# A seven-product gate/up stage with its output sums in PSUM and its engine work in the order of product ends

## The chip, the cores and the metric

The kernel runs on one core of one Trainium2 chip. The metric is device time in microseconds (us), the median of the runs shown. The core has five engines with queues of their own: PE (TensorE, matrix products into PSUM; PEld loads its weights), DVE (VectorE), ACT (ScalarE), POOL (GpSimd) and SP (SyncE), which here only issues DMAs. Engines run in parallel and wait for each other through semaphores.

## The reference

One layer of a hybrid decoder trunk, for 512 prompt tokens and 8 x 4 sample tokens (544 columns in all): adaLN modulation, an input projection that feeds a convolution branch and dilated attention, an output projection, a layer norm, and then the part that matters here:

```python
x = layer_norm(DN_ALPHA * x + (1 + g1) * y, ln1_g, ln1_b)
u = x * (1 + sc2) + sh2
h = (jax.nn.silu(u @ w_gate) * (u @ w_up)) @ w_down
x = layer_norm(DN_ALPHA * x + (1 + g2) * h, ln2_g, ln2_b)
```

`u` is 544 x 1024, `w_gate` and `w_up` are 1024 x 2816, all in fp32.

## The kernel before, in words

Activations lie transposed: 128 channels on the partitions, tokens along the free dimension, in two halves h = 0, 1 of 272 columns (`HC`). For precision each matrix is split into a high part (rounded to fp32r) and a low part (the rest), and a product takes three matmuls: high x high, high x low, low x high. The high part of a weight is made by ACT (`act.copy`, L133 and L1100), the low part by DVE (L134, L1083: weight minus high part). In the profile the weights' tiles are `wr` (raw, loaded by SP at L117), `wh` and `wl`; four raw buffers, three of `wh` and `wl`.

The 2816 columns of gate and up are 22 blocks of 128, called f. A block has a gate weight and an up weight of 8 k-blocks each (`gu[2f]`, `gu[2f+1]`). The f's run in three chunks (0 to 7, 8 to 14, 15 to 21). After each chunk its part of `w_down` is applied, in 8 groups m.

The old way (`mm_group`, L193 on; its matmuls are L199, L200 and L202): 48 matmuls for gate, 48 for up, 96 an f. `gu_evict` (L1012 on) makes silu(gate) x up and splits it into the high and low part of H: a sigmoid on ACT (L1016), two multiplications on DVE (L1018, L1020), a cast on ACT (L1022), a subtraction on DVE (L1024).

The seven-product way (`seven`) treats gate and up, and two halves of u2, as a 2 x 2 block product and does it with seven block products instead of eight, 84 matmuls an f (L1111 to L1113). The units are A11, S1, S2, S3, A12, A22 and S4. A's are blocks of the raw weights; S1 to S4 are sums of blocks, made by POOL (`add_up`, L1073) into three slices of the tile `ss`. The right-hand operands are blocks of u2 and sums of them: S1 and S2 (tile `tb`), S3 and A22 (tile `ta`), made once ahead of the stage from the fp32 tile `tf` by DVE and POOL. The products go into four PSUM buffers, X, Zd, Y and Zc of the pool `pmm`, which has four buffers in all and also holds the old way's results. Three of them are used twice, so the fifth to seventh product add onto what the first to fourth left:

```python
tgt = (X, Zd, Y, Zc, X, Zc, Zd)
after = ((), (p1,), (), (p6,), (p7,), (p2,), (p4,))
```

The steps p1 to p7 and e1, e2 (L1131 on DVE, L1134, L1144, L1150, L1155, L1160 on ACT) add the products up into U2, C22, C21 and C12, which lie in SBUF, and form H. Before, each product is followed in program order by one unit's low part, one POOL sum, one unit's high part (five units ahead, `LEAD`), one step left over from the f before (`rest`) and the steps that belong to that product. The order of the instructions of PE, ACT, DVE and POOL is the program's (a manual schedule), so a step that waits holds up everything behind it on its engine.

f 0 and f 1 are done the old way, half h = 0 first, while layer norm 1 of half 1 (`ln1_gen`, interleaved by `tick`) is still at work, and half 1 afterwards from the same weights (`second`, L1234 to L1236). f 2 is done the old way, f 3 to f 20 by seven products, f 21 the old way. The operands of the seven products are prepared around f 2. In the output projection ahead of it POOL adds high and low part of u2[0] up into `tf` (L1003), and in f 3 and f 4 POOL scales z for the second residual (`idle_work`, L1257). Behind f 21 the weights of the last chunk's `w_down` are split into resident tiles (`wd0`, in the place of `ta` and `tb`), which are allowed once the flag `wd0` is set.

Of the kernel before, what the change touches and what calls it, by code (L numbers as in the profile page):

```python
# [54 lines left out]
def hybrid_step_kernel(ctx: ExitStack, tc: tile.TileContext, I, O):  # L55
# [887 lines left out]
    def ln1_gen(h, stats):  # L943
# [24 lines left out]
        if h == 0:  # L968
            for k in range(8):
                if k % 2 == 0:  # L970
                    yield
# [1 line left out]
                act.activation(out=zk, in_=zk, func=AF.Identity, scale=agb[:, 0, k:k + 1], bias=agb[:, 1, k:k + 1])

    wo = []
    for h in range(2):
        stats = Stats(h, dve)
        for m in range(8):
# [21 lines left out]
            if h == 1 and m == 3:  # L1000
                TF.append(big_tile(0, [128, 4, 4, HC], F32, "tf"))
                for i in range(2):
                    pool.tensor_tensor(out=TF[0][:, i], in0=f32(u2[0][:, 0, 4 * i:4 * i + 4]),  # L1003
                                       in1=f32(u2[0][:, 1, 4 * i:4 * i + 4]), op=ALU.add)
# [59 lines left out]
    def add_up(f, n):  # L1064
        g, u = raw_of(f)
        o = sums[f, n] = own["SS"][:, len(sums) % 3]
        x, y, op = {
            "S1": lambda: (u[:, 0:4], u[:, 4:8], ALU.add),
            "S2": lambda: (sums[f, "S1"], g[:, 0:4], ALU.subtract),
            "S3": lambda: (g[:, 0:4], u[:, 0:4], ALU.subtract),  # L1070
            "S4": lambda: (g[:, 4:8], sums[f, "S2"], ALU.subtract),
        }[n]()
        pool.tensor_tensor(out=o, in0=x, in1=y, op=op)  # L1073
# [4 lines left out]

    def unit_low():
        if los:  # L1080
            f, j = los.pop(0)
# [1 line left out]
            dve.tensor_tensor(out=lo, in0=src_of(f, UNITS[j]), in1=f32(hi), op=ALU.subtract)  # L1083
# [8 lines left out]
    def unit_high(f, j):
        if UNITS[j] == "S4":
            at = (own["S4"][:, 0], own["S4"][:, 1])
        else:
            if j // 2 not in ring:
                ring[j // 2] = (whp.tile([128, 8, 128], F32R, tag="wh", name="wh"), wlp.tile([128, 8, 128], F32R, tag="wl", name="wl"))
            at = tuple(t[:, 4 * (j % 2):4 * (j % 2) + 4] for t in ring[j // 2])
        place[f, j] = at
        act.copy(out=at[0], in_=src_of(f, UNITS[j]))  # L1100
        los.append((f, j))

    def unit(f, j):
        unit_high(f, j)
        unit_low()
# [12 lines left out]
    rest = []  # L1118
    idle_work = []

    def flush():
        while rest:
            rest.pop(0)()

    def seven(f, fi, Hs, coming, hooks):
        X, Zd, Y, Zc = [pmm.tile([128, 512], F32, tag="mm", name="mm") for _ in range(4)]
        s1, U2, C22, C21, C12 = small(tmp, "PT"), small(tmp4, "P"), small(tmp4, "P"), small(tmp, "PT"), small(tmp4, "P")
        sg0, sg1 = small(tmp, "w"), small(tmp, "w")
# [4 lines left out]
        def p1():  # L1133
            act.copy(out=s1, in_=X[:, :HC])  # L1134

        def p6():
            tt(U2, s1, Y[:, :HC], ALU.add)

        def p7():
            tt(C22, U2, Zc[:, :HC], ALU.add)  # L1140
            tt(C22, C22, Zd[:, :HC], ALU.add)

        def p2():
            act.activation(out=sg0, in_=X[:, :HC], func=AF.Sigmoid)  # L1144
            tt(sg0, sg0, X[:, :HC], ALU.mult)

        def p4():
            tt(C21, U2, Zc[:, :HC], ALU.add)
            tt(sg0, sg0, C21, ALU.mult)
            act.copy(out=Hs[0][:, 0, fi], in_=sg0)  # L1150

        def p3():
            tt(Hs[0][:, 1, fi], sg0, f32(Hs[0][:, 0, fi]), ALU.subtract)
            tt(C12, U2, Zd[:, :HC], ALU.add)
            act.activation(out=sg1, in_=C12, func=AF.Sigmoid)  # L1155
# [9 lines left out]
        tgt = (X, Zd, Y, Zc, X, Zc, Zd)
        after = ((), (p1,), (), (p6,), (p7,), (p2,), (p4,))
        for j in range(7):
            product(f, j, tgt[j], j < 4)
            unit_low()
            if j == 0:  # L1170
                add_up(f, "S4")
                if f + 1 in coming:
                    add_up(f + 1, "S1")
# [274 lines left out]
```

## Time and profile before

| what | us |
|---|---|
| median of 3 runs | 1056.51 |
| lowest and highest run | 1055.3, 1056.7 |
| the profiled execution | 1055.41 |
| its span, first to last instruction | 1053.5 |
| f 3 to f 7 by seven products | 679.2 to 737.8 |
| f 8 to f 14 | 785.8 to 867.0 |
| f 15 to f 20 | 909.0 to 977.6 |

The mean granted TensorE clock of the profiled execution is 0.984 of full speed.

Rows of the profile are read so. A group gives line, engine, operation, tile written <- tiles read (buffer numbers left out), the sizes as partitions x elements, and how often; in the view of a line or a tile its durations follow in ns as minimum/median/maximum, in a timeline each row has its start and its duration in us. A row of a window gives its length, the busy time (and number of instructions) of PE, PEld, DVE, ACT and POOL, the granted clock (1.00 is full), the share of the DMA engines and GB/s. A bracket names the idle time of the engine just ahead of the row and who ended it. Matmuls are pipelined and their ends are modelled, so a busy PE may be less than fully at work.

### The profile page before, as it was taken

How to read it: one execution, taken by the hardware profiler on the slowest of the kernel's cores; microseconds unless marked ns; L12 is line 12 of the kernel's file. 1: busy time of each engine (PE TensorE's matmuls, PEld its weight loads, DVE VectorE, ACT ScalarE, POOL GpSimd, SP SyncE). 2: the span in 40 equal slices, each digit the busy share in tenths (PEclk: the TensorE clock that was granted, in tenths of full speed). 3: DMA queues.
4: the chain of work that ended last, by engine and by line, in shares of the span. 5: the costliest groups of instructions: out<-in, count | busy, mean ns of one | idle time of the engine just before them, and what ended most of it. 6: DMA issues, size and time to landing. Idle time of an engine off the chain costs nothing.

```text
span 1053.5 us, 21611 instructions
## 1 busy us (share of the span) xinstructions
PE 988.6 (94%) x8952; PEld 943.6 (90%) x8952; DVE 696.1 (66%) x1181; ACT 461.9 (44%) x910; POOL 260.1 (25%) x295
## 2 busy tenths in 40 slices
PE   4999999999999999999999899799999999998895
PEld 3978999999988989999999898699999899998894
DVE  3422688789786463432229788999449984699487
ACT  3312235445458676444524346544225442345323
POOL 0201010010004402011103645572034421343046
PEclk8999999999999999999999999899999999999998
DMA  9998687696774656899735601056756478457402
GB/s 381 362 386 320 224 312 282 239 343 230 268 299 166 235 211 208 303 370 390 292 141 179 206 1 41 30 191 233 292 204 250 160 285 313 160 182 263 162 10 85
DMA packets 44945, 242.64 MB, mean 230 GB/s; under 512 B 7408, under 2 KB 10736, under 8 KB 37680
## 3 DMA queue, kind: packets, MB, share of 16 engines
q1 hardware_dynamic: 34592, 126.83, 33.5%
q10 hardware_dynamic: 7632, 88.43, 22.6%
q0 software_dynamic: 2624, 26.02, 6.1%
q8 instruction: 70, 1.15, 0.4%
q14 instruction: 27, 0.22, 0.1%
HBM read 231.36 MB, written 97.58 MB: 312 GB/s over the span
## 4 chain that ended last, share of the span: by engine, by line
PE 62%; DVE 23%; ACT 7%; issue 3%; DMA 2%; POOL 2%; ACTq 0%; DVEq 0%; SPq 0%; POOLq 0%
PE mm L199 15%; PE mm L200 14%; PE mm L202 14%; DVE wl L1083 5%; DVE wg L1131 5%; PE mm L1111 2%; PE mm L1112 2%; PE mm L1113 2%; PE od L740 2%; PE Sd L705 2%; PE adaps L334 1%; DMA wr<-in_w_in 1%; DVE mrg L829 1%; ACT wh L1100 1%; PE pt L516 1%
## 5 line engine op out<-in xcount | busy, mean ns | idle before, releaser
L199 PE MATMUL mm<-u,wh 128*128 128x272 f32 x984 | 274.7, 296 | 1.1 <-DVE zsa L993 0.7
L200 PE MATMUL mm<-u,wh 128*128 128x272 f32 x984 | 267.3, 289 | 0.0
L202 PE MATMUL mm<-u,wl 128*128 128x272 f32 x984 | 206.4, 290 | 3.0 <-DVE wl L134 3.0
L199 PEld LDWEIGHTS mm<-u,wh 128*128 128x128 f32 x984 | 186.3, 189 | 15.7 <-issue 11.8
L200 PEld LDWEIGHTS mm<-u,wh 128*128 128x128 f32 x984 | 186.6, 190 | 0.2
L134 DVE TENSOR_TENSOR wl<-wr,wh 128x1024 fp32r<-128x1024 f32 (+2 forms) x98 | 114.0, 1164 | 84.7 <-ACT wh L133 78.3
L202 PEld LDWEIGHTS mm<-u,wl 128*128 128x128 f32 x984 | 155.5, 189 | 3.2 <-DVE wl L134 3.2
L133 ACT CAST wh<-wr 128x1024 fp32r<-128x1024 f32 (+2 forms) x98 | 94.9, 970 | 70.3 <-PE mm L200 50.5
L439 DVE SCALAR_TENSOR_TENSOR convy<-glu,vec,convy 128x512 f32<-128x512 f32 x120 | 95.6, 797 | 2.5
L1073 POOL TENSOR_TENSOR ss<-wr 128x512 f32<-128x512 f32 x36 | 53.1, 1476 | 149.8 <-DMA wr<-in_w_gu 82.3
L200 PE MATMUL mm<-h,wh 128*128 128x272 f32 x240 | 64.7, 288 | 0.0
L199 PE MATMUL mm<-h,wh 128*128 128x272 f32 x240 | 64.5, 286 | 0.0
L1029 DVE SCALAR_TENSOR_TENSOR z<-mm,modT,z 128x272 f32<-128x272 f32 (+1 forms) x48 | 21.7, 479 | 54.1 <-PE mm L202 54.1
L1111 PE MATMUL mm<-ta,wh 128*128 128x272 f32 x144 | 42.9, 298 | 12.9 <-DVE wg L1131 12.7
L1083 DVE TENSOR_TENSOR wl<-wr,wh 128x512 fp32r<-128x512 f32 x54 | 49.4, 920 | 4.6 <-ACT wh L1100 4.3
L1131 DVE TENSOR_TENSOR wg<-wg,mm 128x272 f32<-128x272 f32 x108 | 46.4, 429 | 8.0 <-PE mm L1113 5.9
L637 ACT ACTIVATE qk<-mm,vec 128x272 f32<-128x272 f32 (+1 forms) x48 | 25.9, 627 | 56.5 <-PE mm L202 56.5
L202 PE MATMUL mm<-h,wl 128*128 128x272 f32 x240 | 49.6, 288 | 0.0
L1083 DVE TENSOR_TENSOR wl<-ss,wh 128x512 fp32r<-128x512 f32 x54 | 48.8, 910 | 0.0
L654 POOL DMA_DIRECT2D out_kv<-qk x4 | 2.4, 597 | 182.5 <-ACT qk L637 182.5
L1111 PE MATMUL mm<-u,wh 128*128 128x272 f32 x144 | 42.3, 293 | 4.2 <-DVE sgf L1018 4.2
L199 PEld LDWEIGHTS mm<-h,wh 128*128 128x128 f32 x240 | 45.2, 188 | 0.0
(325 smaller groups left out, 2601.3 us busy)
## 6 DMA issues: line engine op xcount, KB each, us to landing
out_s<-in_c ACTq DMA_DIRECT2D x32, 2044.0 KB, 9.4
wr<-in_w_in SPq DMA_DIRECT2D x60, 512.0 KB, 6.3
wr<-in_w_gu SPq DMA_DIRECT2D x44, 512.0 KB, 4.7
KT<-in_kt SPq DMA_DIRECT2D x24, 792.0 KB, 7.1
VV<-in_vv SPq DMA_DIRECT2D x24, 768.0 KB, 7.5
gb<-in_w_ada POOLq DMA_DIRECT2D x8, 2048.0 KB, 16.6
out_s<-in_c ACTq DMA_DIRECT2D x8, 2032.0 KB, 9.3
ga<-in_w_ada SPq DMA_DIRECT2D x8, 1024.0 KB, 17.5
```

Source lines behind the costliest of these rows:

```text
L133: act.copy(out=hv, in_=raw)
L134: dve.tensor_tensor(out=lv, in0=raw, in1=hv.bitcast(F32), op=ALU.subtract)
L199: pe.matmul(ps[h][:, :HC], lhsT=hi[:, k], rhs=A[h][:, 0, k], start=(k == 0), stop=False)
L200: pe.matmul(ps[h][:, :HC], lhsT=hi[:, k], rhs=A[h][:, 1, k], start=False, stop=False)
L202: pe.matmul(ps[h][:, :HC], lhsT=lo[:, k], rhs=A[h][:, 0, k], start=False, stop=(k == nk - 1))
L439: dve.scalar_tensor_tensor(out=o, in0=src, scalar=sc, in1=o, op0=ALU.mult, op1=ALU.add)
L637: act.activation(out=o, in_=src, func=AF.Identity, bias=V("b_in", col))
L1029: dve.scalar_tensor_tensor(out=zz[:, :n1], in0=ps[:, :n1], scalar=modT[:, 5, m, 0:1], in1=zz[:, :n1], op0=ALU.mult, op1=ALU.add)
L1073: pool.tensor_tensor(out=o, in0=x, in1=y, op=op)
L1083: dve.tensor_tensor(out=lo, in0=src_of(f, UNITS[j]), in1=f32(hi), op=ALU.subtract)
L1111: pe.matmul(ps[:, :HC], lhsT=hi[:, k], rhs=B[:, 0, k], start=(first and k == 0), stop=False, skip_group_check=not first)
L1131: dve.tensor_tensor(out=o, in0=a, in1=b, op=op)
```

## The change

It touches the gate/up stage and what is prepared for it.

- One more f in the old way: f 3 goes through `mm_group` and `gu_evict`; the seven products do f 4 to f 20.
- C22, C21 and C12 move from SBUF into PSUM buffers of the pools `ps_s` and `ps_o`.
- The high parts of A11 and S1 are copied a second time, into PSUM (`twice`, one buffer of `ps_t`), and the low part is computed from that copy.
- S2 and S3 lie side by side and are split by one copy and one subtraction of 1024 columns.
- The order inside `seven` is written out: behind each product stand the steps that its end allows, the unit of f + 1 whose buffer it frees among them. The steps left over from an f (`c12`, `lo0`, `m1`, `hi1`, `lo1`, `a22`) are placed by name in the next one.
- `tf`'s part of u2[0] comes from ACT (a second scaling of z in `ln1_gen`) instead of POOL, and there is one more `yield` ahead of it. t3 and t4 are made by DVE instead of POOL. The scaling of z that was POOL's `idle_work` is done by ACT (`keep`) around f 2 and f 3.
- In the last chunk the flag `wd0` is set ahead of f 21, and the left-over steps of f 20 (`flush`) come behind f 21's gate group. The units of the first f of a chunk are spread a little differently over the down groups m = 5 to 7.

The diff, cut to its core:

```diff
         u2[h] = A
         if h == 0:
+            yield
             for k in range(8):
                 if k % 2 == 0:
                     yield
                 zk = stats.zt(k)
+                act.activation(out=TF[0][:, k // 4, k % 4], in_=zk, func=AF.Identity, scale=G9[:, k, 0:1], bias=B9[:, k, 0:1])
                 act.activation(out=zk, in_=zk, func=AF.Identity, scale=agb[:, 0, k:k + 1], bias=agb[:, 1, k:k + 1])
...
                 TF.append(big_tile(0, [128, 4, 4, HC], F32, "tf"))
-                for i in range(2):
-                    pool.tensor_tensor(out=TF[0][:, i], in0=f32(u2[0][:, 0, 4 * i:4 * i + 4]),
-                                       in1=f32(u2[0][:, 1, 4 * i:4 * i + 4]), op=ALU.add)
...
+        act.copy(out=hi, in_=src_of(f, n))
+        if n == "S2":
+            place[f, 2], place[f, 3] = (hi[:, 0:4], lo[:, 0:4]), (hi[:, 4:8], lo[:, 4:8])
+        else:
+            place[f, j] = (hi, lo)
+        seen = f32(hi)
+        if twice:
+            seen = ps_t.tile([128, 4, 128], F32, tag="t", name="hip")
+            act.copy(out=seen, in_=f32(hi))
+
+        def low():
+            dve.tensor_tensor(out=lo, in0=src_of(f, n), in1=seen, op=ALU.subtract)
...
+        product(f, 0, X, True)
+        later("c12")
+        later("lo0")
+        later("m1")
+        lo = unit_high(f, "S4")
+        lo()
+        later("a22")
+        if nxt:
+            add_up(f + 1, "S1")
+        Zd = bank()
+        product(f, 1, Zd, True)
+        s1 = small(tmp, "PT")
+        act.copy(out=s1, in_=X)
+        later("hi1")
+        if nxt:
+            lo = unit_high(f + 1, "A11", True)
+            later("lo1")
+            lo()
+            add_up(f + 1, "S2")
+            add_up(f + 1, "S3")
+        else:
+            later("lo1")
+        Y = bank()
+        product(f, 2, Y, True)
+        U2 = small(tmp4, "P")
+        if nxt:
+            lo = unit_high(f + 1, "S1", True)
+        tt(U2, s1, Y, ALU.add)
+        if nxt:
+            lo()
+            add_up(f + 1, "S4")
...
+        product(f, 3, Zc, True)
+        C22 = ps_s.tile([128, 512], F32, tag="s", name="c22")[:, :HC]
+        U3 = small(tmp4, "P")
+        tt(U3, U2, Zc, ALU.add)
+        tt(C22, U3, Zd, ALU.add)
+        if nxt:
+            unit(f + 1, "S2")
+        product(f, 4, X, False)
+        act.activation(out=sg0, in_=X, func=AF.Sigmoid)
+        tt(sg0, sg0, X, ALU.mult)
+        if nxt:
+            unit(f + 1, "A12")
...
+        product(f, 5, Zc, False)
+        C21 = ps_o.tile([128, 512], F32, tag="o", name="c21")[:, :HC]
+        tt(C21, U2, Zc, ALU.add)
+        tt(C21, sg0, C21, ALU.mult)
+        if nxt:
+            rest["a22"] = unit_high(f + 1, "A22")
+        act.copy(out=Hs[0][:, 0, fi], in_=C21)
+        product(f, 6, Zd, False)
+        C12 = ps_s.tile([128, 512], F32, tag="s", name="c12")[:, :HC]
+        def c12():
+            tt(C12, U2, Zd, ALU.add)
             act.activation(out=sg1, in_=C12, func=AF.Sigmoid)
+        def lo0():
+            tt(Hs[0][:, 1, fi], C21, f32(Hs[0][:, 0, fi]), ALU.subtract)
+        def m1():
             tt(sg1, sg1, C12, ALU.mult)
+            tt(C22, sg1, C22, ALU.mult)
...
-        wg = [f for f in range(k0, k1) if 3 <= f < 21]
+        wg = [f for f in range(k0, k1) if 4 <= f < 21]
...
             pg = mm_group(w_next(2), u2, 8)
+            for i in range(2):
+                gu_evict({1: second[2 * i]}, {1: second[2 * i + 1]}, H, i)
+            dve.tensor_tensor(out=T["S1"][:, 1], in0=tf[:, 0], in1=f32(T["S1"][:, 0]), op=ALU.subtract)
+            prep_to(pos["use"] + 2)
+            pu = mm_group(w_next(2), u2, 8)
+            dve.tensor_tensor(out=T["S2"][:, 1], in0=tf[:, 3], in1=f32(T["S2"][:, 0]), op=ALU.subtract)
             TA = big_tile(0, [128, 2, 2, 4, HC], F32R, "ta")
             T["S3"], T["A22"] = TA[:, 0], TA[:, 1]
             act.copy(out=T["S3"][:, 0], in_=t3)
-            gu_evict({1: second[0]}, {1: second[1]}, H, 0)
+            keep(0)
+            keep(1)
             dve.tensor_tensor(out=T["S3"][:, 1], in0=t3, in1=f32(T["S3"][:, 0]), op=ALU.subtract)
             act.copy(out=T["A22"][:, 0], in_=t4)
+            keep(2)
+            keep(3)
             own["SS"] = one.tile([128, 3, 4, 128], F32, tag="vT", name="ss")
+            gu_evict(pg, pu, H, 2)
+            prep_to(pos["use"] + 2)
...
+            pg = mm_group(w_next(2), u2, 8)
             dve.tensor_tensor(out=T["A22"][:, 1], in0=t4, in1=f32(T["A22"][:, 0]), op=ALU.subtract)
...
+            unit(f, "A11")
+            unit(f, "S1")
+            add_up(f, "S4")
             pu = mm_group(w_next(1), u2, 8)
+            unit(f, "S2")
+            gu_evict(pg, pu, H, 3)
+            unit(f, "A12")
+            rest["a22"] = unit_high(f, "A22")
...
         if j == 2:
+            res["wd0"] = [big_tile(i, [128, 4, 8, 128], F32R, f"wd0{i}") for i in (0, 1)]
+            flags.add("wd0")
+            pg = mm_group(w_next(), u2, 8)
             flush()
-            pg = mm_group(w_next(), u2, 8)
             pu = mm_group(w_next(), u2, 8)
             gu_evict(pg, pu, H, nf - 1)
             copies(0.8)
-            res["wd0"] = [big_tile(i, [128, 4, 8, 128], F32R, f"wd0{i}") for i in (0, 1)]
-            flags.add("wd0")
```

More of the change, by code (lines that the diff above doesn't have):

```diff
@@ L1051, in hybrid_step_kernel @@
     UNITS = ("A11", "S1", "S2", "S3", "A12", "A22", "S4")
-    LEAD = 5
-    rw, place, los, sums, T, own = {}, {}, [], {}, {}, {}
+    rw, place, sums, T, own = {}, {}, set(), {}, {}
     def rhs_of(n):
@@ L1088, in unit_low, with unit @@
                 load_more()
-                assert pos["prep"] == i
+                assert pos["prep"] == i and (f, "S4") in sums
                 pos["prep"] = i + 2
[L1092 to L1105, printed above, removed]
+        return low
+    def unit(f, n):
+        unit_high(f, n)()
     def product(f, j, ps, first):
@@ L1116, in small, with later @@
         return pool_.tile([128, NT if tag == "w" else 512], F32, tag=tag, name="wg")[:, :HC]
-    rest = []
-    idle_work = []
+    rest = {}
+    def later(name):
+        if name in rest:
+            rest.pop(name)()
     def flush():
[L1122 to L1128, printed above, removed]
+        for n in list(rest):
+            later(n)
@@ L1130, in tt, with seven, bank @@
+    def seven(f, fi, Hs, nxt, hooks):
+        def bank():
+            return pmm.tile([128, 512], F32, tag="mm", name="mm")[:, :HC]
         def tt(o, a, b, op):
             dve.tensor_tensor(out=o, in0=a, in1=b, op=op)
[L1133 to L1154, printed above, removed]
+        sg0, sg1 = small(tmp, "w"), small(tmp, "w")
+        X = bank()
+        product(f, 0, X, True)
[3 more added lines that the diff above has]
+        lo = unit_high(f, "S4")
@@ L1165, in seven @@
[L1165 to L1173, printed above, removed]
-            elif j in (1, 3) and f + 1 in coming:
-                add_up(f + 1, ("S2", "S3")[j // 2])
-            n = j + LEAD
-            if n < 7:
-                unit_high(f, n)
-            elif f + 1 in coming:
-                unit_high(f + 1, n - 7)
-            if rest:
-                rest.pop(0)()
-            for g in after[j]:
-                g()
-            if j in hooks:
-                hooks[j]()
-            if idle_work and j > 2:
-                idle_work.pop(0)()
@@ L1189, in seven, with hi1, lo1 @@
-        rest.extend((p3, e1, e2))
+            tt(C22, sg1, C22, ALU.mult)
+        def hi1():
+            act.copy(out=Hs[1][:, 0, fi], in_=C22)
+        def lo1():
+            tt(Hs[1][:, 1, fi], C22, f32(Hs[1][:, 0, fi]), ALU.subtract)
+        rest.update(c12=c12, lo0=lo0, m1=m1, hi1=hi1, lo1=lo1)
         pos["use"] += 2
@@ L1218, in hybrid_step_kernel, with keep @@
             prep_to(pos["use"] + 1)
-            pool.tensor_tensor(out=t3, in0=tf[:, 3], in1=tf[:, 2], op=ALU.subtract)
+            def keep(k):
+                zk = z[:, k, HC:NT]
+                act.activation(out=zk, in_=zk, func=AF.Identity, scale=agb[:, 0, k:k + 1], bias=agb[:, 1, k:k + 1])
             for i in range(2):
```

81 lines of the change are left out of this document (39 added, 42 removed).

## The prediction, made blind

> **What bounds the kernel now.** I read the page first, then the busy times of stretches that I cut at the changed stage, then single lines and tiles in it. The profiled execution spans 1053.5 us and took 1055.41; the median of the three runs is 1056.51, 0.1% more, so I sum on the profile and take the difference from the median. About 0.2% (2.1 us) is what a measurement of this kernel can tell from no change.
>
> ```profile
> span 1053.5 us, 21611 instructions
> PE 988.6 (94%) x8952; PEld 943.6 (90%) x8952; DVE 696.1 (66%) x1181; ACT 461.9 (44%) x910; POOL 260.1 (25%) x295
> ```
>
> ```profile
> core 0: us, PE busy (x) PEld busy (x) DVE busy (x) ACT busy (x) POOL busy (x), PEclk, DMA share, GB/s
> 679.20:737.80 58.60, 55.28 (x420) 54.62 (x421) 53.38 (x88) 28.30 (x58) 28.53 (x24) 0.97 0.55 197
> 785.80:867.00 81.20, 75.67 (x591) 74.38 (x590) 74.82 (x123) 38.63 (x80) 30.95 (x22) 1.00 0.61 218
> 909.00:977.60 68.60, 64.54 (x506) 63.66 (x505) 62.84 (x105) 33.23 (x68) 24.60 (x18) 1.00 0.60 206
> 977.60:989.70 12.10, 12.10 (x98) 12.04 (x97) 2.91 (x7) 1.66 (x5) 0.00 (x0) 1.00 0.35 127
> 989.70:1005.00 15.30, 12.64 (x87) 12.27 (x86) 9.62 (x14) 6.96 (x9) 0.00 (x0) 0.89 0.46 150
> ...
> ```
>
> ```profile
> 844.10:856.40 12.30, 10.87 (x86) 10.65 (x85) 11.84 (x19) 5.57 (x12) 5.77 (x4) 1.00 0.70 251
> ```
>
> The first three windows are the seven-product f's of the three chunks (5, 7, 6 of them). The fourth is f 21 in the old way: 96 matmuls in 12.1 us, 0.1254 each, nothing else late. Seven products are 84 matmuls, so 10.5 us if PE never waits; the windows give 11.7, 11.6 and 11.4 an f. The single f from 844.1 takes 12.3, PE loses 1.4 there and DVE is busy 11.84. So in this stage DVE is the bound, against a page in which PE leads.
>
> ```profile
> L1131 DVE TENSOR_TENSOR wg<-wg,mm x108: 422/426/441, 685.5 to 978.1; 128x272 f32<-128x272 f32 x108
> L1131 DVE TENSOR_TENSOR wg<-wg x54: 426/442/1537, 690.8 to 979.6; 128x272 f32<-128x272 f32 x54
> L1083 DVE TENSOR_TENSOR wl<-wr,wh x54: 676/688/1777, 674.2 to 968.8; 128x512 fp32r<-128x512 f32 x54
> L1073 POOL TENSOR_TENSOR ss<-wr x36: 1279/1430/2322, 670.3 to 960.6; 128x512 f32<-128x512 f32 x36
> ```
>
> ```profile
> 846.29 2.98 DVE L1131 TENSOR_TENSOR wg<-wg 128x272 f32<-128x272 f32 x2
> ```
>
> ```profile
> 845.84 1.69 POOL L1073 TENSOR_TENSOR ss<-wr 128x512 f32<-128x512 f32 x1 [3.81 <-DMA wr<-in_w_gu]
> 847.61 1.37 POOL L1073 TENSOR_TENSOR ss<-ss,wr 128x512 f32<-128x512 f32 x1
> ```
>
> Durations are min/median/max in ns. A DVE op with one input in PSUM (wg<-wg,mm) never leaves 0.42 to 0.44 in 108 cases; with both inputs in SBUF it reaches 1.54, and a weight's low half 1.78. The two timelines show why: two such multiplications take 2.98 us because each ends where a POOL addition does (847.5, 849.0). Twelve of the 18 DVE ops of an f have both inputs in SBUF, and POOL adds four times an f.
>
> **The change part by part.** *Steady f's.* After the change 4 of 17 DVE ops (the low halves of S4, A22, A12 and of S2 with S3, one op of 1024) read SBUF twice. C22, C21, C12 and second copies of A11's and S1's high halves lie in PSUM.
>
> ```profile
> L1100 ACT CAST wh<-wr x54: 609/620/631, 671.4 to 968.2; 128x512 fp32r<-128x512 f32 x54
> L519 ACT COPY PT<-pt x24: 572/587/682, 178.5 to 410.1; 128x512 f32<-128x512 f32 x24
> L1155 ACT ACTIVATE wg<-wg x18: 431/432/433, 694.3 to 978.6; 128x272 f32<-128x272 f32 x18
> L133 ACT CAST wo<-wr x8: 1036/1045/1054, 565.0 to 590.6; 128x1024 fp32r<-128x1024 f32 x8
> L134 DVE TENSOR_TENSOR h<-wr,h x2: 1212/1218/1225, 636.7 to 653.4; 128x1024 fp32r<-128x1024 f32 x2
> ```
>
> DVE undisturbed: 11 ops of 0.43, 5 of 0.68, one of 1.22, together 9.35: under 10.5. ACT gets two copies more (2 x 0.62); its sum is 4 halves of 0.62, two copies, one of 1.05, six ops of 0.4: 7.2, beside PE. The copy into PSUM is in no row. Nearest are SBUF to SBUF 0.62 and PSUM to SBUF 0.59; I take 0.62; up to 1.2 it stays off the path, because S1's low half has over 1 us before it is missed. ps_t has one buffer, so S1's second copy waits on ACT for A11's low half; behind it stands the copy of S2 and S3, which waits for POOL anyway.
>
> What is late next is a ring through POOL. The S1 addition of f+1 overwrites the slice from which S4 of f is read, so it waits for S4's low half. From that end on: A22's low half 0.60 (POOL waits, since both read SBUF; next ops on one engine start 0.08 before the last ends), three additions at 1.31 and 0.2 of handoffs 4.13, the copy of S2 and S3 1.05 + 0.06, their low half 1.22 + 0.06, sg0 times X 0.35, A12's low half 0.60, C21 0.35 and 0.49, C12 0.35, sigmoid 0.49, two multiplications 0.98, S4's low half 0.60. Sum 11.3 an f. The addition's 1.31 is chosen: 1.28 is its undisturbed minimum, 1.43 its median with two weight inputs; with 1.31 the same laying end to end of before's queues gives 10.5, 11.4, then 12.2, and 10.5 for the last f of a chunk: 81.2 and 69.0 for the windows of 81.2 and 68.6. A chunk enters with its units ready, which puts the ring over a microsecond ahead, and it loses 0.8 an f: two f's of 10.5, a third of 10.9; the last, with no next f, 10.8. Seven f's: 10.5 + 10.5 + 10.9 + 3 x 11.3 + 10.8 = 76.6 against 81.2, so -4.6. Six: 65.3 against 68.6, so -3.3. Bounds: 10.6 if the slack of POOL is better than I think, 12.2 if the S4 addition always gets in ahead of S2's low half. The S4 addition and A22's copy of a chunk's first f move into the down groups m = 6 and 7: nothing, beside 5 to 6 us of PE each.
>
> [...]
>
> *First chunk: one more f in the old way.* It adds 12 matmuls (1.5 us), but what counts is when f 4 starts its products.
>
> ```profile
> 662.30:674.80 12.50, 9.03 (x50) 8.63 (x48) 10.93 (x11) 5.77 (x10) 6.51 (x4) 0.73 0.12 43
> 674.80:679.20 4.40, 0.20 (x2) 0.00 (x0) 4.40 (x6) 1.20 (x3) 3.03 (x3) 1.00 0.00 0
> 679.20:682.60 3.40, 3.39 (x15) 3.39 (x16) 3.26 (x7) 2.59 (x6) 2.02 (x2) 0.50 0.00 0
> ```
>
> ```profile
> 660.71 1.29 DVE L1227 TENSOR_TENSOR tb<-tf,tb 128x1088 fp32r<-128x1088 f32 x1
> 661.97 3.54 DVE L1228 TENSOR_TENSOR tb<-tf,tb 128x1088 fp32r<-128x1088 f32 x1
> 665.43 1.21 DVE L134 TENSOR_TENSOR wl<-wr,wh 128x1024 fp32r<-128x1024 f32 x1
> ```
>
> ```profile
> 691.38 0.29 PE L1111 MATMUL mm<-u,wh 128*128 128x272 f32 x1
> ```
>
> ```profile
> L973 ACT ACTIVATE z<-z,agb x8: 601/602/609, 623.0 to 634.1; 128x272 f32<-128x272 f32 x8
> ```
>
> Before, PE loses 3.5 us to a low half queued behind L1228, which POOL's t4 held for 2.3, waits 4.4 more for the units, and runs at half clock after each idle stretch (0.50 in the third window). f 4 begins at 691.38. After: t3 and t4 are DVE ops of 1.29 and POOL blocks nothing. From 657.2 (L1227's 660.71 less two ops, less 0.8 that t3 on POOL cost) run three of 1.29 at 1.25, the S2 copy 1.1, gu5's copy 1.05 and low half 1.21: it ends at 664.3, not 666.6, and f 2's up group, 45 matmuls on, at 669.9. But f 3's gate group needs the PSUM buffers of f 2's gate group (pmm has four, all held), so it waits for f 2's first two multiplications (L1018), and these for a sigmoid that stands on ACT behind what the change puts there. DVE: two evictions of h = 1 (six ops, two casts and handoffs) 3.6, S1 low, gu6 low, S2 low 3.6, to 671.5. ACT then: S3 copy 1.1 (it overwrites tf, so after S2 low), two keeps of z 1.1, A22 copy 1.1, two keeps 1.1, sigmoid 0.4, to 676.1. The multiplication ends at 676.6. PE idles 6.7, then 96 matmuls 12.0, then half clock on about 26 of them, 2.6. f 4 begins at 691.3: nothing won, nothing lost. Bounds: 688 (no half clock, keeps overlap) to 694.5. Its four f's take 10.6 + 11.0 + 11.3 + 10.8 = 43.7, to 735.1 against 737.8: -2.7.
>
> [...]
>
> *The sums of u2 off POOL.* Two POOL additions go, eight ACT ops of 0.6 come, and one extra yield puts them later.
>
> ```profile
> L1003 POOL TENSOR_TENSOR tf<-u x2: 2525/2528/2531, 616.1 to 623.6; 128x1088 f32<-128x1088 f32 x2
> ```
>
> ```profile
> 616.48 2.44 DVE L950 TENSOR_TENSOR u<-u2a,u 128x272 fp32r<-128x272 f32 x1 [0.53 <-ACT u L960]
> ```
>
> ```profile
> 635.34 0.43 ACT L873 ACTIVATE lnsq<-z 128x272 f32<-128x272 f32 x1 [0.61 <-DVE z L995]
> ```
>
> DVE loses 2.0 to each addition (0.44 alone, 2.44 here), so 4 come back there. On ACT, eight ops at 0.51 start to start, 4.1, now stand ahead of the last square, 635.34. The two cancel: 0, from -1 to +4 if only the ACT side shows.
>
> *The end of the gate/up stage.* The weights of the first down groups are split during f 21 instead of behind it.
>
> ```profile
> 991.01 0.85 ACT wd L133
> ...
> 991.89 1.10 DVE wd L134
> ...
> 993.03 0.48 PE mm L202
> ```
>
> The window from 989.7 holds 84 matmuls of down, 10.5 us, and 2 others, and takes 15.3. Split early, these rows leave the path; H of f 21 is needed only 18 matmuls in, 2.25 us, and its casts end at 991.01, 1.3 after f 21's last matmul. So -4.7, half clock included. Cover: f 21's 12 us.
>
> One call of copies falls away; the last piece moves from f 20 to f 21, off the path.
>
> Sum: -4.6 - 3.3 - 2.7 + 0 - 4.7 = -15.3. Profile 1040.1, median 1041.2.
>
> **The rivals.** *PE becomes the bound* (10.6 an f): the chunks win another 1.3, 2.6 and 1.9: 1035.4. For: POOL's undisturbed 1.28 and DVE's 9.35. Against: the ring's sum.
>
> *Another wait takes the place of the old*, 12.2 an f: the S4 addition ahead of S2's low half, or the weights. Row:
>
> ```profile
> wr<-in_w_gu SPq DMA_DIRECT2D x44, 512.0 KB, 4.7
> ```
>
> The POOL row at 845.84 above waited 3.81 for such a load, so a landing can be far slower than this median; a shorter period leaves it less time. Then the two later chunks lose 0.3 and 0.7, f 4 to 7 (45.2) win 1.2, the end 4.7: 1051.3.
>
> *Slower: POOL stops every DVE op, PSUM or not.* DVE's 9.35 less 17 overlaps of 0.08, 8.0, and four additions, 5.2, then follow one another: 13.2 an f. With 10.7 for a first and 10.8 for a last f, seven take 87.5 (+6.3), six 74.3 (+5.7), four 47.9 (+1.4); with the end's -4.7 that is 1065.2. It turns slower from 12.6 an f on (11 such f's). Against it stand 108 cases of wg<-wg,mm within 20 ns.
>
> *The change does not do what it says* (A11's and S1's low halves still stop, up to 1.31 each, with 1 us of slack): 12 an f, within the second rival.
>
> **How the numbers follow.** Forecast 0.52, own range 1036 to 1046; PE bound 0.20; another wait 0.17; slower 0.05; the rest 0.06 is the ACT side of u2's sums with half clock twice on top of the second rival, 1055 to 1059. The range 1032 to 1052 holds the second rival and the bounds above and leaves out about 0.17: the slower case, the last 0.06 and the far ends. Faster by over 0.2%: 0.52 + 0.20 + 0.17 + 0.01 = 0.90; the same 0.04; slower 0.06.
>
> **What would show it.** Right: PE's idle time ahead of L1111 that DVE wg ends, in all,
>
> ```profile
>   DVE wg L1131: 28.2, 22
> ```
>
> (both PE rows, us and times) falls to a few us; low halves of A11 and S1 stay at 0.68; the S1 addition starts right behind the low halves of S4 and A22; f's of 11.3 in mid chunk; PE idle 6 to 7 us ahead of f 3's gate group, released by sgf; no gap at the first down group. Wrong: f's of 12 with POOL waiting for DMA, or PSUM readers beyond 0.5 us; lnps later than before.

## The result and the profile after

The changed kernel takes 1040.48 us, the median of four runs from 1038.72 to 1041.41; the kernel before ran at 1056.61 beside it. The ratio is 0.984, with a 95% interval from 0.982 to 0.987. The profiled execution took 1039.63 us and spans 1037.9, which is 15.6 less than the 1053.5 of before.

The page of the changed kernel, first lines; the columns are as before:

```profile
span 1037.9 us, 21539 instructions
...
PE 989.9 (95%) x8964; PEld 946.5 (91%) x8964; DVE 647.1 (62%) x1156; ACT 480.8 (46%) x931; POOL 233.5 (23%) x279
```

DVE lost 49 us of busy time with 25 operations fewer, which would be 2 us for each, and the longest DVE operation of this stage takes 1.29 in the changed kernel: the operations that stayed became shorter. ACT gained 19 us.

The busy times by stretch, cut at the same events as before (f 3's gate group, the seven-product f's of the three chunks, f 21, the first down groups of the last chunk):

```profile
core 0: us, PE busy (x) PEld busy (x) DVE busy (x) ACT busy (x) POOL busy (x), PEclk, DMA share, GB/s
...
672.00:678.80 6.80, 0.45 (x5) 0.23 (x3) 3.56 (x5) 4.69 (x8) 2.37 (x2) 0.89 0.22 77
678.80:693.30 14.50, 14.50 (x96) 14.50 (x97) 7.56 (x12) 6.41 (x12) 2.70 (x3) 0.81 0.12 37
693.30:736.80 43.50, 43.17 (x339) 42.53 (x338) 33.91 (x65) 24.85 (x48) 16.39 (x12) 1.00 0.54 192
784.80:860.30 75.50, 75.09 (x591) 74.29 (x590) 59.70 (x117) 44.17 (x85) 32.86 (x24) 1.00 0.65 235
902.30:966.70 64.40, 64.20 (x506) 63.64 (x505) 50.93 (x99) 37.73 (x72) 27.36 (x20) 1.00 0.61 226
966.70:978.80 12.10, 12.10 (x99) 12.10 (x98) 5.50 (x11) 3.54 (x7) 0.00 (x0) 1.00 0.61 205
978.80:989.40 10.60, 10.60 (x86) 10.60 (x86) 7.52 (x12) 5.08 (x7) 0.00 (x0) 1.00 0.47 165
```

Read down the first number behind each stretch. Seven f's take 75.5 us instead of 81.2, six take 64.4 instead of 68.6, the first down groups 10.6 instead of 15.3: 5.7, 4.2 and 4.7 us. The first chunk's four seven-product f's end at 736.8 instead of 737.8, 1.0 earlier, although f 4 starts later, at 693.3 instead of 691.4. These four are the whole 15.6. PE is now busy in 99.5% of the second chunk's stage, where it was at 93%; DVE went from 92% to 79%.

Single lines of the changed kernel (min/median/max in ns), L1136 being the element operations, L1098 the low halves, L1071 POOL's additions:

```profile
L1136 DVE TENSOR_TENSOR c<-wg,c x34: 445/445/447, 705.0 to 971.5; 128x272 f32<-128x272 f32 x34
L1136 DVE TENSOR_TENSOR wg<-wg,c x17: 436/439/440, 706.5 to 971.1; 128x272 f32<-128x272 f32 x17
```

```profile
L1098 DVE TENSOR_TENSOR wl<-wr,hip x14: 686/688/690, 697.7 to 949.8; 128x512 fp32r<-128x512 f32 x14
L1098 DVE TENSOR_TENSOR wl<-ss,hip x14: 686/687/691, 700.1 to 951.9; 128x512 fp32r<-128x512 f32 x14
```

```profile
  DVE wg L1136: 3.6, 13
```

No element operation reaches 0.45 us any more, where the slowest took 1.54, and the low halves that read a high half in PSUM stay within 5 ns of each other. The last fence is the idle time of PE ahead of a product that a DVE operation ended: 3.6 us in 13 places, where it was 28.2 in 22.

### The profile page after: what moved, and what is told of

Its sections match the earlier page's. It is cut to its first block, busy times and chain, and to the rows that moved or that the text cites. A ratio compares the mean times of both kernels' runs of the same rounds, so it can differ in the third digit from the quotient of the medians.

```text
span 1037.9 us, 21539 instructions
## 1 busy us (share of the span) xinstructions
PE 989.9 (95%) x8964; PEld 946.5 (91%) x8964; DVE 647.1 (62%) x1156; ACT 480.8 (46%) x931; POOL 233.5 (23%) x279
## 4 chain that ended last, share of the span: by engine, by line
PE 65%; DVE 11%; issue 8%; ACT 7%; POOL 5%; DMA 4%; ACTq 0%; DVEq 0%; POOLq 0%
PE mm L199 16%; PE mm L200 15%; PE mm L202 15%; POOL ss L1071 3%; DMA wr<-in_w_gu 2%; PE mm L1114 2%; PE mm L1115 2%; PE mm L1116 2%; PE od L740 2%; PE Sd L705 2%; PE adaps L334 1%; PE pt L516 1%; DVE mrg L829 1%; DMA wr<-in_w_in 1%; DVE wl L134 1%
## 5 line engine op out<-in xcount | busy, mean ns | idle before, releaser
L199 PE MATMUL mm<-u,wh 128*128 128x272 f32 x1016 | 285.0, 298 | 6.4 <-DVE sgf L1017 6.4
L200 PE MATMUL mm<-u,wh 128*128 128x272 f32 x1016 | 277.0, 290 | 0.0
L202 PE MATMUL mm<-u,wl 128*128 128x272 f32 x1016 | 213.7, 290 | 0.5 <-DVE wl L134 0.5
L199 PEld LDWEIGHTS mm<-u,wh 128*128 128x128 f32 x1016 | 193.7, 191 | 20.9 <-issue 11.0
L200 PEld LDWEIGHTS mm<-u,wh 128*128 128x128 f32 x1016 | 193.9, 191 | 0.4
L202 PEld LDWEIGHTS mm<-u,wl 128*128 128x128 f32 x1016 | 161.3, 190 | 0.7 <-DVE wl L134 0.7
L133 ACT CAST wh<-wr 128x1024 fp32r<-128x1024 f32 (+2 forms) x100 | 97.0, 972 | 66.5 <-PE mm L200 50.5
L1071 POOL TENSOR_TENSOR ss<-wr 128x512 f32<-128x512 f32 x34 | 50.2, 1476 | 189.0 <-DVE s L1098 90.2
L1087 ACT CAST wh<-ss 128x512 fp32r<-128x512 f32 (+1 forms) x34 | 28.4, 835 | 43.6 <-POOL ss L1071 30.6
L199 PEld LDWEIGHTS mm<-h,wh 128*128 128x128 f32 x240 | 45.2, 188 | 0.0
L200 PEld LDWEIGHTS mm<-h,wh 128*128 128x128 f32 x240 | 45.1, 188 | 0.0
L509 ACT ACTIVATE P<-P,st 128x256 f32<-128x256 f32 x64 | 31.2, 489 | 28.3 <-DVE st L503 25.8
L1114 PE MATMUL mm<-ta,wh 128*128 128x272 f32 x136 | 40.4, 297 | 0.9 <-DVE wg L1136 0.8
L200 PE MATMUL mm<-mrg,wo 128*128 128x272 f32 x128 | 37.9, 296 | 1.8 <-DVE mrg L829 1.7
```

What stands on the lines that cost most here:

```text
L133: act.copy(out=hv, in_=raw)
L199: pe.matmul(ps[h][:, :HC], lhsT=hi[:, k], rhs=A[h][:, 0, k], start=(k == 0), stop=False)
L200: pe.matmul(ps[h][:, :HC], lhsT=hi[:, k], rhs=A[h][:, 1, k], start=False, stop=False)
L202: pe.matmul(ps[h][:, :HC], lhsT=lo[:, k], rhs=A[h][:, 0, k], start=False, stop=(k == nk - 1))
L509: act.activation(out=p[:, a:b], in_=p[:, a:b], func=AF.Exp, bias=st[:, kd, s, hh, 0:1], accum_out=st[:, kd, s, hh, 1:2])
L1087: act.copy(out=hi, in_=src_of(f, n))
```

## Experiments

Each kernel is the changed kernel with one edit (the last two with several), timed against the kernel before on the same chip. Ratios are to the kernel before; the changed kernel's own is 0.984 (0.982 to 0.987), and differences of medians are against its 1040.5. The kernel before took 1057.6 to 1058.2 beside the experiments and 1056.6 beside the changed kernel, so a difference of medians can be off by over a microsecond: by the ratios the gains come out up to 1 us larger and the losses up to 1.3 smaller.

**Is it the place of the operands? All in SBUF.** C22, C21 and C12 go back to SBUF, and the second copies of A11's and S1's high halves go, so seven more operations of an f have both inputs in SBUF; the order of the work stays.

```diff
-        C22 = ps_s.tile([128, 512], F32, tag="s", name="c22")[:, :HC]
+        C22 = small(tmp4, "P")
-        C21 = ps_o.tile([128, 512], F32, tag="o", name="c21")[:, :HC]
+        C21 = small(tmp, "PT")
-        C12 = ps_s.tile([128, 512], F32, tag="s", name="c12")[:, :HC]
+        C12 = small(tmp4, "P")
-            lo = unit_high(f + 1, "A11", True)
+            lo = unit_high(f + 1, "A11")
-            lo = unit_high(f + 1, "S1", True)
+            lo = unit_high(f + 1, "S1")
```

> Changed kernel with its order of work, but C22, C21, C12 in SBUF and no second copies of the high halves of A11 and S1 (four operations of an f read PSUM less; two ACT copies go). Theory: DVE operations with two SBUF inputs stop beside POOL's additions again: f's of about 12.2 us in mid chunk, 1050 to 1053 us, and low halves of A11 and S1 that reach over 1 us. Rival: the order of the work and the merged operation of S2 and S3 made the gain: f's of 10.8 to 11.3, 1039 to 1043 us.

It took 1059.3 us, ratio 1.001 (1.000 to 1.003): 18.9 more than the changed kernel, more than the theory gave, and the whole gain gone with wins elsewhere (the first down groups) still in it. Three f's in the middle of the second chunk, first in the changed kernel, then in this one:

```profile
816.80:849.70 32.90, 32.49 (x254) 31.85 (x254) 26.02 (x52) 19.96 (x39) 16.42 (x12) 1.00 0.61 217
```

```profile
827.80:864.50 36.70, 32.51 (x255) 31.85 (x254) 35.70 (x52) 16.97 (x33) 18.06 (x12) 1.00 0.57 197
```

The same 52 DVE operations are busy 35.7 us instead of 26.0. An f takes 12.2, as expected; what the theory missed is the second f of a chunk, which takes 14.8, 14.2 and 12.7. With these operands in SBUF the new order gains nothing. The converse, the old order with the operands in PSUM, was not run: the place is shown to be needed, not to be enough.

**Which of them: the low halves or the sums?** Two halves of that edit, apart.

> Changed kernel without the second copies of the high halves of A11 and S1: their two low halves read SBUF twice, C22, C21 and C12 stay in PSUM, and two ACT copies (0.59 each, one of them on the ring) go. Theory: what counts is which operations lie beside POOL's additions, and these two do (A11's beside the S1 addition, S1's beside that of S3): each stops for up to 1.3 us, f's of 11.8 to 12.5, 1050 to 1057 us. Rival: the number of operations with two SBUF inputs counts, and these are two of seven that all-SBUF adds: 1040 to 1045 us; below 1040 if the copy on ACT was the dearer way.

> Changed kernel with C22, C21 and C12 in SBUF and the second copies of the high halves kept in PSUM: five more operations of an f read SBUF twice. Theory (place decides): most of them lie between the last product and the low half of S4, when POOL waits for that low half; only the low half of the second H (842.86 us, beside the S1 addition) stops, at most 0.9 an f: 1042 to 1048 us. Rival (number decides): five of the seven operations of all-SBUF's 19 us come back: 1051 to 1056 us.

Without the second copies: 1047.8 us, ratio 0.990 (0.989 to 0.992), 7.3 more. With the three C's in SBUF: 1041.1, ratio 0.985 (0.983 to 0.986), no difference. So place decides and not number, but the sizes were missed: for the low halves the theory's was too high and the rival's too low, and the C's came out 0.9 under their theory's range. The f's of the kernel without copies take 11.6 to 11.8. Its low halves, DVE first, then POOL's additions in the same f:

```profile
812.78 1.43 DVE L1098 TENSOR_TENSOR wl<-wr,wh 128x512 fp32r<-128x512 f32 x1
814.48 1.42 DVE L1098 TENSOR_TENSOR wl<-ss,wh 128x512 fp32r<-128x512 f32 x1
```

```profile
811.99 1.67 POOL L1071 TENSOR_TENSOR ss<-wr 128x512 f32<-128x512 f32 x1 [5.50 <-DVE s L1098]
813.73 1.62 POOL L1071 TENSOR_TENSOR ss<-ss,wr 128x512 f32<-128x512 f32 x1
815.31 1.73 POOL L1071 TENSOR_TENSOR ss<-wr 128x512 f32<-128x512 f32 x1
```

Both engines pay: the low halves take 1.43 instead of 0.69, and POOL's additions 1.6 to 1.7 instead of 1.3. Of the five operations on the C's four lie where POOL waits some 5.5 us for S4's low half, and nothing meets them. The fifth, the low half of the second H, lies beside the S1 addition; with the C's in SBUF it takes 1.52 to 1.54 instead of 0.44 in 11 of the 17 f's:

```profile
842.98 1.53 DVE L1136 TENSOR_TENSOR h<-wg,h 128x272 fp32r<-128x272 f32 x1
```

That costs 0.1 us an f, because DVE was idle for 1.10 a little later, ahead of S1's low half, and that idle time takes most of it up. The two halves cost 7.3 and 0.6 apart and 18.9 together. In the kernel with all in SBUF the same 11 operations stop, but there is no idle time behind them: A11's low half then takes 1.78 instead of 1.43, and the low half of S2 and S3 comes to lie beside the S4 addition and takes 1.78 instead of 1.23.

```profile
845.18 1.78 DVE L1098 TENSOR_TENSOR wl<-wr,wh 128x512 fp32r<-128x512 f32 x1
...
849.38 1.78 DVE L1098 TENSOR_TENSOR wl<-ss,wh 128x1024 fp32r<-128x1024 f32 x1
```

In these rows a low half of 128x512 with both inputs in SBUF takes 1.42 to 1.78 us where it starts while an addition runs, and A22's, which starts ahead of one, 0.68 (at 811.83 in the kernel without copies). With one input in PSUM, the 28 of the changed kernel take 0.686 to 0.691.

**What is the ring of 11 us?** The next f's S1 low half goes behind U2 + Zc.

```diff
         tt(U2, s1, Y, ALU.add)
-        if nxt:
-            lo()
-            add_up(f + 1, "S4")
...
         tt(U3, U2, Zc, ALU.add)
+        if nxt:
+            lo()
+            add_up(f + 1, "S4")
         tt(C22, U3, Zd, ALU.add)
```

> Changed kernel with one move on DVE and POOL: the low half of the next f's S1 (and the S4 addition behind it) comes behind U2 + Zc instead of ahead of it. Theory: the ring that sets 10.8 to 11.05 us in mid chunk runs S4 low, S1 addition 1.29 to 1.68, two copies on ACT 1.25, S1 low 0.69, U2 + Zc 0.43, sixth product; with the last but one off it the f's take 10.55 and the three chunks win 1.1, 1.5 and 1.1: about 1037 us. Rival: the ring of the prediction (three additions in a row, then the copy and low half of S2 and S3) stands right behind it and keeps 10.8 to 11: 1040 to 1041 us.

It took 1036.7 us, ratio 0.981 (0.978 to 0.984), 3.8 less by the medians, though the two intervals overlap. The f's take 10.59 (84 matmuls at 0.1254 are 10.53) until the fifth of a chunk; the last two of the second chunk take 11.06 and 11.03, the last of the third 11.03. So the theory has the place where PE waits, but not what sets 11 us. S4's low half in three f's of this kernel:

```profile
796.17 0.69 DVE L1098 TENSOR_TENSOR s<-ss,s 128x512 fp32r<-128x512 f32 x1
807.22 0.69 DVE L1098 TENSOR_TENSOR s<-ss,s 128x512 fp32r<-128x512 f32 x1
818.27 0.69 DVE L1098 TENSOR_TENSOR s<-ss,s 128x512 fp32r<-128x512 f32 x1
```

They lie 11.05 apart, while PE starts the same f's at 793.30, 803.89 and 814.48, 10.59 apart. A loop that takes 11.05 while PE runs at 10.59 doesn't go through PE: it is the rival's ring, the one of the prediction. From the second f of a chunk on it is 10.8 to 11.1 long in both kernels, and the move leaves it as it is. What the move changes is how far PE gets ahead before it meets the ring: in the f's in which PE waits, S4's low half ends 5.2 us into the f here and 3.7 in the changed kernel. In the last f's a low half of the down weights stands ahead of U2 + Zc as well. The stages won 0.9, 0.5 and 0.3 us, 1.7 of the expected 3.7; f 4 starts 1.2 earlier in this profile for nothing that the edit does, and the rest is within the scatter of the runs.

**The stall ahead of f 3's gate group.** f 2's sigmoids and first multiplications, taken out of `gu_evict` as `gate`, go right behind the evictions of the second halves.

```diff
-            dve.tensor_tensor(out=T["S1"][:, 1], ...
+            sg = gate(pg)
             prep_to(pos["use"] + 2)
             pu = mm_group(w_next(2), u2, 8)
+            dve.tensor_tensor(out=T["S1"][:, 1], ...
+            gu_evict(pg, pu, H, 2, sg)
             dve.tensor_tensor(out=T["S2"][:, 1], ...
...
-            gu_evict(pg, pu, H, 2)
```

> Changed kernel (1040.5 us), with f 2's sigmoid and first multiplication put right behind the evictions of the second halves, ahead of the low halves and of the copies of S3 and A22. Theory: the 6.64 us that PE waits ahead of f 3's gate group is queue order alone; the stall goes to under 1 us, with it the half clock behind it (22 matmuls at 0.23 instead of 0.125, 2.3 us), f 4 starts at 684.5 to 687 instead of 693.3: 1031.5 to 1034 us. Rival: the units of f 4 (low halves of S3 and A22, the sums on POOL) come no earlier, so the wait moves to f 4's first products; f 4's third product starts no earlier than 693: 1037 us or more.

1038.0 us, ratio 0.981 (0.979 to 0.984): 2.5 less, with intervals that overlap, where the theory had 6.5 to 9. The stall is gone from where it was, but PE now waits at f 3's up group, and neither the theory nor the rival had named that:

```profile
682.14 0.39 PE L199 MATMUL mm<-u,wh 128*128 128x272 f32 x1 [3.33 <-ACT wh L133]
```

```profile
679.05 1.08 ACT L1286 CAST ta<-t 128x1088 fp32r<-128x1088 f32 x1
680.04 1.12 ACT L1253 ACTIVATE z<-z,agb 128x272 f32<-128x272 f32 x2
681.06 1.03 ACT L133 CAST wh<-wr 128x1024 fp32r<-128x1024 f32 x1
```

The second fence is ACT's queue: the up weights' high half (L133) stands behind the same copies and scalings that had held the sigmoid. PE then waited once more, ahead of the matmul that needs its low half; by the matmul starts the two waits are 3.6 and 1.9. f 4 starts at 691.5 instead of 693.3.

**The sums of u2, later on ACT.** The eight ACT operations go behind the second half's square root, the scaling of z's first half into the first chunk's down groups.

> Changed kernel with the eight ACT operations that make the sums of u2 moved from ahead of the last square to behind the square root of the second half, and the scaling of z's first half moved into the first chunk's down groups. Theory: the last matmul of the statistics (638.86 us in the changed kernel, PE idle 5.6 ahead of it) waits for the last square behind these operations; it comes at about 634.4, the half clock behind it goes too, and all later work moves up by 4 to 5.5 us: 1035 to 1036.5 us. Rival: the queue of ACT ahead of f 3's gate group takes the gain back, since the same operations then stand before u2's second half: 1039.5 to 1041 us.

1034.1 us, ratio 0.978 (0.975 to 0.980): 6.4 less and 0.9 under the theory's range, the largest gain of these single edits. The last statistics matmul, in the changed kernel and here:

```profile
638.86 0.82 PE L923 MATMUL lnps<-lnq,ones 128*128 128x272 f32 x1 [5.25 <-POOL lnq L882]
```

```profile
635.69 0.50 PE L923 MATMUL lnps<-lnq,ones 128*128 128x272 f32 x1 [0.22 <-POOL lnq L882]
```

PE's idle of 5.25 is 0.22, and f 4 starts at 689.6 instead of 693.3, although the output projection began 1.5 later in this profile (571.5 against 570.0). The wait ahead of f 3's gate group stays at 6.35 us, so the rival is out.

**The sums of u2, back on POOL.**

> Changed kernel with the sums of u2 made on POOL again by two additions, from the high and low halves, and without the eight ACT operations. The prediction's term for this part of the change was 0, from -1 to +4. Theory: of the two sides only ACT's counts, as the last statistics matmul came at 638.86 against 636.91 before: putting it back wins 1.5 to 2.5 us, 1038 to 1039 us. Rival: DVE loses its 4 us beside POOL's additions again and is then late by as much: 1040 to 1043 us.

1037.9 us, ratio 0.982 (0.980 to 0.983), 2.6 less by the medians; the intervals of the two ratios overlap, so this leans to the theory and no more. In its profile the output projection began 1.5 later, as above, and the last statistics matmul comes at 639.4; from one to the other it is 67.9 us, against 68.9 in the changed kernel and 67.1 before, so 1.0 of the 1.8 that the change had added there is gone again. From 608 to 650 us PE lost, in matmul starts later than 0.125 behind the one before, 4.8 us before the change, 8.6 in the changed kernel, 6.4 here, and 2.9 with the later place.

**The tail undone.** The weights of the first down groups are split behind f 21 again.

> Changed kernel with the weights of the first down groups split behind f 21 again. Theory: the prediction's term, 4.7 us (idle 2.3 and 0.9 ahead of the first down group's first and third matmul, half clock on the rest): 1044.5 to 1046 us. Rival: f 21's eviction now comes otherwise, and part of the split hides beside it: 1041 to 1043 us.

1045.2 us, ratio 0.988 (0.986 to 0.989), 4.8 more by the medians, near the term of 4.7. In its profile the stretch from f 21's last matmul to the 82nd of the down groups takes 16.4 us, against 15.0 before and 10.3 in the changed kernel, as 24 matmuls run at half clock there and 16 did before: the matmul between the two waits takes 0.43 (at 981.35), where it took 0.28 before (at 992.14). The waits are back where they were:

```profile
980.95 0.59 PE L199 MATMUL mm<-h,wd 128*128 128x272 f32 x1 [2.46 <-ACT wd L133]
...
982.08 0.59 PE L202 MATMUL mm<-h,wd 128*128 128x272 f32 x1 [0.31 <-DVE wd L134]
```

**f 3 in seven products again.**

```diff
-        wg = [f for f in range(k0, k1) if 4 <= f < 21]
+        wg = [f for f in range(k0, k1) if 3 <= f < 21]
```

(and without f 3's two groups and its eviction)

> Changed kernel with f 3 in the seven-product way again, all else as it is. The prediction held that one more f in the old way wins and loses nothing as far as f 4's start goes. Theory: f 3's first product then waits for the sums on POOL and for ACT's copies and scalings until about 682 to 683, runs its first products at half clock, and f 4 starts at 694 to 696 instead of 693.3: 1041 to 1043.5 us. Rival: PE has 12 matmuls less (1.5 us) and f 3's units are as early as f 3's up group was: f 4 at 691 to 692, 1038 to 1039.5 us.

1040.3 us, ratio 0.983 (0.982 to 0.985): no difference. f 3 starts at 681.6 behind 9.3 us of idle PE, and f 4 at 694.0 against 693.3. So the theory had f 4's start right; the time is 0.7 below its range. One more f in the old way is worth nothing here.

**The gains together.** The three moves, f 3's up weights split right behind f 2's eviction, A11's low half behind U2, and all scalings of z in the down groups.

> Changed kernel with the three moves together: f 2's gate multiplication early (and, as that run left PE waiting 3.6 and 1.9 us for f 3's up weights behind ACT's queue, these weights split right behind f 2's eviction), the sums of u2 behind the second half's square root, U2 and U2 + Zc ahead of the low halves of A11 and S1; all sixteen scalings of z go into the first chunk's down groups. Theory: the gains add: 6.4 (sums of u2), 3.8 to 4.5 (U2 + Zc), 8.7 (stall of 6.6 and half clock 2.3): 1020 to 1023 us. Rival: f 4's sums and low halves then come last and keep f 4's third product waiting: 1025 to 1031 us.

1029.9 us, ratio 0.973 (0.972 to 0.975). The gains didn't add: the time is in the rival's range, but the wait is not the rival's; it is at f 4's first product:

```profile
684.88 0.59 PE L1114 MATMUL mm<-u,wh 128*128 128x272 f32 x1 [4.80 <-DVE sgf L1012]
```

It is the pattern of f 2 once more: a PSUM buffer that f 3's first multiplication holds, and this stands on DVE behind the low half of S2 and S3, which waits for POOL. POOL's sums there, and the first of them in the next kernel:

```profile
676.52 2.27 POOL L1071 TENSOR_TENSOR ss<-wr 128x512 f32<-128x512 f32 x1 [28.50 <-DVE ta L1277]
678.87 1.60 POOL L1071 TENSOR_TENSOR ss<-ss,wr 128x512 f32<-128x512 f32 x1
680.43 1.71 POOL L1071 TENSOR_TENSOR ss<-wr 128x512 f32<-128x512 f32 x1
```

```profile
676.17 1.29 POOL L1071 TENSOR_TENSOR ss<-wr 128x512 f32<-128x512 f32 x1 [28.50 <-DVE ta L1277]
```

The next kernel's edit against this one, cut to its core:

```diff
...
             pg = mm_group(w_next(2), u2, 8)
-            dve.tensor_tensor(out=T["A22"][:, 1], ...
...
-            unit(f, "A11")
-            unit(f, "S1")
-            add_up(f, "S4")
+            lo = unit_high(f, "A11", True)
+            sg = gate(pg)
+            lo()
             pu = mm_group(w_next(1), u2, 8)
+            unit_high(f, "S1", True)()
+            add_up(f, "S4")
+            gu_evict(pg, pu, H, 3, sg)
             unit(f, "S2")
-            gu_evict(pg, pu, H, 3)
+            dve.tensor_tensor(out=T["A22"][:, 1], ...
...
```

> The combined kernel of before (1029.9 us) with f 3's eviction and f 4's first units in another order: in the combined kernel f 4's first product waits 5.1 us for a PSUM buffer that f 3's first multiplication holds behind the low half of S2 and S3, and the next product waits 1.4 more. Here f 3's sigmoids and first multiplications come ahead of f 4's units, A11's and S1's first low halves read a copy in PSUM, the low half of A22's sum moves behind S2 and S3, and in every f C22 is made ahead of S1's low half. Theory (queue order again): f 4 starts at 679.8 to 681 instead of 684.9, its first f takes 10.6 to 11 instead of 12.0: 1023 to 1025.5 us. Rival: POOL's three sums in a row (2.3, 1.6 and 1.7 us there) are the bound and the wait moves to f 4's third product: 1026 to 1029 us.

1026.4 us, ratio 0.971 (0.969 to 0.972): 3% below the kernel before and 1.4% below the changed one. f 4 starts at 679.6, 13.8 us earlier than in the changed kernel, with no idle ahead of it: the theory's place. The time is 0.9 above the theory's range and at the low end of the rival's. POOL's sums are at 1.3 again, and one matmul of the third product starts 0.8 behind the one before, so the rival's wait isn't there. The theory's first f of 10.6 to 11 isn't there either: f 4 to f 7 take 11.6, 11.4, 10.9 and 10.8. They start with their units just made and have no lead to use up; that reason is argued, not tried. PE is busy in 96% of the span.

## Why the prediction held, step by step

It said 1041.2 and it was 1040.5; profile against profile, 1040.1 forecast and 1039.6 measured. The reason was right. That the total comes within 0.7 us is partly luck, because two errors in its terms cancel.

- **DVE operations with two SBUF inputs stop beside POOL's additions, those with one in PSUM don't.** Shown for the operations of this stage: all-SBUF costs 18.9 us with the order kept, and its low halves reach 1.78 us and its element operations 1.53. The rival in which POOL stops every DVE operation is out, since the 28 low halves that read PSUM keep 0.686 to 0.691 us while additions run beside them.
- **Steady f's: the right ring, sized too long.** Forecast 76.6 and 65.3 for the windows, measured 75.5 and 64.4. The pattern is the forecast one: in the second chunk two f's at PE's pace (10.60 and 10.59), one of 10.78 in which the lead runs out, then 11.06, 10.83 and 11.05 where 11.3 stood, and 10.6 for the last where 10.8 stood. The term that was mis-sized is "A22's low half 0.60 (POOL waits, since both read SBUF", with the three additions behind it. One f of the changed kernel, on DVE, POOL, ACT and PE:

```profile
841.66 0.68 DVE L1098 TENSOR_TENSOR s<-ss,s 128x512 fp32r<-128x512 f32 x1
...
845.48 0.69 DVE L1098 TENSOR_TENSOR wl<-ss,hip 128x512 fp32r<-128x512 f32 x1 [1.10 <-POOL ss L1071]
846.09 0.43 DVE L1136 TENSOR_TENSOR wg<-wg,mm 128x272 f32<-128x272 f32 x1
...
847.84 1.23 DVE L1098 TENSOR_TENSOR wl<-ss,wh 128x1024 fp32r<-128x1024 f32 x1 [0.84 <-ACT wh L1087]
...
852.71 0.68 DVE L1098 TENSOR_TENSOR s<-ss,s 128x512 fp32r<-128x512 f32 x1
```

```profile
842.42 1.68 POOL L1071 TENSOR_TENSOR ss<-wr 128x512 f32<-128x512 f32 x1 [5.50 <-DVE s L1098]
844.18 1.30 POOL L1071 TENSOR_TENSOR ss<-ss,wr 128x512 f32<-128x512 f32 x1
845.43 1.28 POOL L1071 TENSOR_TENSOR ss<-wr 128x512 f32<-128x512 f32 x1
```

```profile
846.75 1.05 ACT L1087 CAST wh<-ss 128x1024 fp32r<-128x1024 f32 x1 [1.37 <-POOL ss L1071]
```

```profile
846.57 0.39 PE L1114 MATMUL mm<-ta,wh 128*128 128x272 f32 x1 [0.20 <-DVE wg L1136]
```

S4's low half ends at 842.34, and each step of the ring starts where the one before ends. By the profile the S1 addition doesn't wait for A22's low half to end, as the prediction had it. It starts right behind S4's, takes 1.68 beside A22's, and the third addition ends at 846.71, 4.37 behind S4's low half where 0.60 and 4.13 stood. The copy and the low half of S2 and S3 then take 2.36 (forecast 2.39), and DVE's queue to the end of the next S4 low half, at 853.39, takes 4.32 (forecast 4.21). Together that is 11.05 where 11.3 stood.

A second step fails too: "up to 1.2 it stays off the path, because S1's low half has over 1 us before it is missed". Once the lead is gone, S1's low half is what PE meets first: U2 + Zc (846.09) stands behind it, and PE's sixth product waits 0.20 for that. The run with S1's low half moved shows its worth: PE then meets the ring 1.5 us later in an f, and the stages win 1.7 in all.
- **First chunk.** The stall was forecast at 6.7 us and is 6.64 from one matmul start to the next, and what released it is what was named. ACT's queue in the changed kernel:

```profile
673.85 1.10 ACT L1275 CAST ta<-t 128x1088 fp32r<-128x1088 f32 x1 [3.15 <-DVE tb L1272]
674.86 1.12 ACT L1248 ACTIVATE z<-z,agb 128x272 f32<-128x272 f32 x2
675.88 1.08 ACT L1279 CAST ta<-t 128x1088 fp32r<-128x1088 f32 x1
676.87 1.12 ACT L1248 ACTIVATE z<-z,agb 128x272 f32<-128x272 f32 x2
677.88 0.66 ACT L1015 ACTIVATE sgf<-mm 128x272 f32<-128x272 f32 x2
```

```profile
678.79 0.59 PE L199 MATMUL mm<-u,wh 128*128 128x272 f32 x1 [6.35 <-DVE sgf L1017]
```

The granted clock of 0.81 in the window from 678.8 is the half clock behind it: 23 matmul starts 0.23 apart, 2.4 us, where 2.6 was forecast for 26 matmuls. Before, the 26 behind the idle time that ends at 666.70 took 5.87, which is 2.6 more than at 0.1254 each. All of this lies 2.0 us later than forecast, and f 4 with it, at 693.3 instead of 691.3; its four f's took 43.45 for 43.7.
- **The sums of u2: the term that failed.** The prediction let DVE's 4 us and ACT's 4.1 cancel. They don't: DVE's side did come 3.4 earlier (the first statistics matmul at 632.88 instead of 636.29), but the last one waits, through a sum on POOL, for ACT's last square, and came at 638.86 instead of 636.91:

```profile
638.04 0.76 POOL L882 TENSOR_TENSOR lnq<-lnq,lnsq 128x272 f32<-128x272 f32 x1 [3.64 <-ACT lnsq L873]
```

The later of two chains counts, not their sum. The 2.0 lie inside the bounds given, and "lnps later than before" had been named as a sign of it.
- **The tail** was 4.7, right to 0.1 by the window; the undone run gives 4.8 by the medians, 6.1 by the stretch in its profile.
- **Sum:** the gains of the three stages were forecast 1.1, 0.9 and 0.3 too small, and the cost in the sums of u2 2.0 too small. The second rival's 1051.3 is a slip of 0.3: its own terms add up to 1051.6.

An input in PSUM costs these operations nothing that the rows show: the multiplications with both inputs in SBUF take 0.443 us in the all-SBUF kernel, and 0.439 and 0.445 with one in PSUM.
